# Operands of a Strassen-Winograd projection formed from PSUM, and four steps near them moved, in a one-core decoder block

## The chip, the cores and the metric

The kernel runs on one core of a Trainium2 chip. The metric is the device time of one execution in microseconds (us), as the median of several runs. The core has five engines that run side by side: TensorE (PE, matrix products into PSUM), VectorE (DVE, elementwise), ScalarE (ACT, functions and copies), GpSimd (POOL, elementwise, which in this kernel works on SBUF alone) and SyncE (SP, which here only issues loads and stores). Each engine works through its own instructions in order; they wait for one another through semaphores.

## The reference

One decoder block on x of 1024 positions by 1024 channels, all in float32:

```
u  = RMSNorm(h) * norm_mix_w
P  = u @ w_in                 # [gate_a | gate_s | B_a | C_a | v_a | z | xBC | dt]
A  = (B_a * causal_dwconv3(C_a * v_a)) @ w_a_out
S  = GroupRMSNorm(SSD(silu(conv4(xBC)), softplus(dt + dt_bias)) * silu(z)) @ w_s_out
h  = h + (sigmoid(gate_a) * A + sigmoid(gate_s) * S) @ w_o
v  = RMSNorm(h) * norm_ffn_w
h  = h + (silu(causal_dwconv3(v @ W_1) + b) * (v @ W_3)) @ w_down
out = RMSNorm(h) * final_norm_w
```

SSD is the Mamba-2 scan in chunks of 128 positions: decays are the running sum of dt * a within a chunk, and each chunk uses exp of differences of them.

## The kernel before

**Products.** Every float32 matrix is split in two parts that PE takes quickly: `hi`, the value rounded by an ACT cast, and `lo`, the rest, by a subtraction on DVE or POOL (`split`, L146 to L149). A product of two such operands is three chains of matmuls (`product`, L261): for one 128 x 512 output 12 matmuls of 128 x 512.

**Strassen-Winograd.** The projections by `w_in` (operand U) and by `w_up` (operand V) are computed in pairs of output tiles with seven products in place of eight. The left operand, transposed, is cut into four blocks: A11 and A12 (first 512 positions, lower and upper 512 channels), A21 and A22 (last 512 positions). Four sums are wanted besides A11, A12 and A22:

```
S1 = A21 + A22    S2 = S1 - A11    S3 = A11 - A21    S4 = A12 - S2
```

Each of these is a pair of tiles (hi, lo) of 128 x 4 x 512 (`operand`, L197), filled one row tile of 128 positions at a time. The weights get four sums as well (T1 to T4, `Pair.operands`, L318, all on POOL).

**Filling.** `u_norm(t)` (L436) scales the row tile `xs[t]` in place: ACT squares, DVE makes the mean, POOL the power -0.5, DVE multiplies by it and by the norm weights `nw`, which a DMA has broadcast to all partitions (L433, queued on SP behind the first two rows of x). `fill_first` (L206, t = 0 to 3) transposes eight blocks on PE into two PSUM tiles, splits each from PSUM into A11 and A12, and copies both back into `xs[t]` for later (`keep`, L212). `fill_second` (L214, t = 4 to 7) is a generator in stages: it transposes the row tile, forms S1 with an ACT copy and a DVE addition, copies A21 to SBUF (L236), splits S1 and A22; then S2 = S1 - A11 (L240) and S3 = A11 - A21 (L242), both on SBUF; then S4 (L250), the split of S3 on POOL and the split of S4 on DVE. For V nothing was kept: POOL adds hi and lo of A11 and A12 up again (`whole`, L229).

All operands of U do not fit beside the rows of x: there are 14 large buffers, and S3's and S4's tiles take those of the rows, once these have been read for the last time.

**The order of the work.** The whole program is unrolled; a planner orders the instructions of each engine at build time by a model of their times, in the order of the code where several are ready. `tc.issue_after(i)` ties the instructions traced inside it behind `i` on the same engine. U's phase runs: first halves; the products for dt; second halves; three gate pairs (`head`, L502 to L515) whose first products need A11 and A12 alone; then `then(p)` for each (L679 to L684), s2, s4 and s3 of the pairs interleaved. `so_far` (L328) takes a product out of PSUM, with DVE for these pairs (u2, u3). There is one buffer for T2 (`t2`, L122).

**Decays.** `decays` (L533) makes the decays in a chain on DVE and ACT in [heads, positions], stores them by SP to DRAM for broadcasts, and transposes them on PE into `tk` (L586 to L594). It runs ahead of `BEFORE`, six pairs; its row pool is closed behind it and the pool `ssp` of the SSD chunks opens. A chunk (`ssd_chunk`, L702) loads `m`, the broadcast decays, by a DMA that ACT issues, and makes tables of it with `tk` on ACT (L724). Its stages are called between the products of `BESIDE`, 31 pairs.

**V.** `s_out(1, ..)` (the product by `w_s_out`) calls `fill_first` for V beside its products; `fill_second` runs from the last `out_proj` into the first pairs of the MLP (L1045 to L1094). Then come 22 MLP pairs and the product by `w_down`.

Of the kernel before, what the change touches and what calls it, by code (L numbers as in the profile page):

```python
# [15 lines left out]
P = 128  # L16
# [19 lines left out]
LO_DVE = ("t1", "b22")  # L36

NWAT = 1

# [26 lines left out]
def tile_block(  # L66
# [126 lines left out]


    COMBOS = ("a11", "a12", "a22", "s1", "s2", "s3", "s4")

# [8 lines left out]

    def fill_first(A, v, t, name, keep=False):  # L206

        ts = slice(t * P, (t + 1) * P)
        for pt, c, h in zip(transposed(v, name), ("a11", "a12"), halves):
            split(pt, A[c][0][:, :, ts], A[c][1][:, :, ts], dve)  # L210
            if keep:
                act.copy(blocks(v[:, h]), pt)  # L212

    def fill_second(A, v, t, name, first=None, own=None):  # L214


        pts = transposed(v, f"{name}{t}", mm_tile)
        ts = slice(t * P, (t + 1) * P)

        def put(c, val, eng=dve):  # L220
            split(val, A[c][0][:, :, ts], A[c][1][:, :, ts], eng)

        def whole(c, nm):

            if first is not None:
                return blocks(first[:, halves[c == "a12"]])
            hi, lo = (f32(a[:, :, ts]) for a in A[c])
            o = blocks(c2(f"{nm}{name}{t}"))
            pool.tensor_tensor(o, hi, lo, op=ALU.add)  # L229
            return o  # L230

        s1, a21 = (blocks(v[:, h]) for h in halves)
        act.copy(s1, pts[1])
        dve.tensor_tensor(s1, s1, pts[0], op=ALU.add)
        put("s1", s1)
        act.copy(a21, pts[0])  # L236
        put("a22", pts[1])
        yield
        a11 = whole("a11", "a11")
        dve.tensor_tensor(s1, s1, a11, op=ALU.subtract)  # L240
        put("s2", s1)
        dve.tensor_tensor(a21, a11, a21, op=ALU.subtract)  # L242
        if first is None:
            put("s3", a21, pool)
            yield
        a12 = whole("a12", "a12")
        s4 = a12 if own is None else blocks(
            own.tile([P, HALF], F32, tag="own", name=f"own{name}{t}", bufs=4)
        )
        dve.tensor_tensor(s4, a12, s1, op=ALU.subtract)  # L250
        if first is not None:
            yield
            put("s3", a21, pool)
        put("s4", s4)
        yield
# [5 lines left out]
    def product(ps, c, w, start=True, stop=True, held=False):  # L261


        hi, lo = (t.rearrange("p (k c) -> p k c", k=4) for t in w)
        n = 0
        for wt, ct in ((hi, c[0]), (hi, c[1]), (lo, c[0])):
            for k in range(4):
                pe.matmul(  # L268
                    ps, wt[:, k, :], ct[:, k, :],
                    start=(start and n == 0), stop=(stop and n == 11), skip_group_check=held,  # L270
                )
                n += 1

    class Pair:
# [27 lines left out]
        def first(self, late=False, hold=True, place=None):  # L302


            self.started = True
            p = self.prod("a11", self.r1[:, :HALF], "b11")
            d1 = None if self.d1 is None else self.d1[:, :HALF]
            if place is None:
                place = (d1 if hold else c2(f"m1{self.name}"), d1)
            self.m1, self.c11 = place  # L310
            act.copy(self.m1, p)
# [6 lines left out]
        def operands(self):  # L318
# [3 lines left out]
            self.t1, self.t2, self.t3, self.t4, self.b22 = b11, t2(f"t2{name}"), b12, b21, b22  # L322
            pool.tensor_tensor(self.t1, b12, b11, op=ALU.subtract)
            pool.tensor_tensor(self.t2, b22, self.t1, op=ALU.subtract)
            pool.tensor_tensor(self.t3, b22, b12, op=ALU.subtract)
            pool.tensor_tensor(self.t4, b21, self.t2, op=ALU.subtract)

        def so_far(self, o, c, w, nm):  # L328

            if self.hold:  # L330
                act.copy(o, self.prod(c, w, nm, self.u))
            else:
                dve.tensor_tensor(o, self.m1, self.prod(c, w, nm), op=ALU.add)
                self.m1 = o

# [87 lines left out]
    zeros = const([P, 4], "zeros")  # L423
    dve.memset(zeros, 0.0)
    nw = s4("nw_mix")[:, :DM]
    xs = []
    for t in range(0, NCH, 2):
        xt = big_tile(f"x{t}", shape=(P, 2, DM))
        for i in range(2):
            sp.dma_start(xt[:, i, :], x[(t + i) * P : (t + i + 1) * P, :])  # L430
            xs.append(xt[:, i, :])
            if t + i == NWAT:
                sp.dma_start(nw, norm_mix_w.unsqueeze(0).to_broadcast([P, DM]))  # L433
    U = operand("u")
# [63 lines left out]
    for t in range(4, 8):  # L498
        u_norm(t)
    fills = [fill_second(U, xs[t], t - 4, "u", xs[t - 4], cur["row"]) for t in range(4, 8)]  # L500
    stage(fills[:2])
    for j in range(0, 6, 2):  # L502
# [25 lines left out]
    wns = const([P, NH // 2], "wns", ssd_norm_w)  # L528
    ones = const([P, P], "ones")
    dve.memset(ones, 1.0)  # L530


    def decays(ps):  # L533
# [50 lines left out]
        )  # L584

        tkf = tk.rearrange("p a c q h -> p (a c q h)")  # L586
        for b, arrs in enumerate(((ac, dtv), (dd,))):
            w = len(arrs) * QT
            pt = sd_tile(f"tkp{b}")[:, :w]
            for a, arr in enumerate(arrs):  # L590
                for c in range(2):
                    o = (2 * a + c) * P
                    pe.transpose(pt[:, o : o + P], arr[:, c * P : (c + 1) * P], ident)
            act.copy(tkf[:, b * HALF : b * HALF + w], pt)  # L594


# [82 lines left out]
    for i, p in enumerate(head):  # L679
# [170 lines left out]

    for item in BEFORE:
        run(*item)
    clock[0] = 0
    for item in BESIDE:
# [178 lines left out]
    def fill_beside(j):  # L1033
        if j % 2 == 0:
            fill_first(V, v_norm(j // 2), j // 2, f"v{j // 2}")

    V = operand("v")
    mg = s_out(1, ys1, fill_beside)
    load_x(1)
    V.update(operand("v", False))  # L1040
    def v_second(t):
        v = v_norm(t)
        return fill_second(V, v, t - 4, "v")

# [50 lines left out]


    scf = mkpool("scf", 1)
    two = {}
# [259 lines left out]
```

## Time and profile before

| | |
|---|---|
| runs | 1977.09, 1970.45, 1973.09 us; median 1973.09 |
| profiled execution | 1974.46 us, of which the profile's span is 1972.7 |
| granted clock of TensorE, mean | 0.989 |
| DVE / ACT / POOL busy | 65% / 49% / 63% |
| first transposition on PE | at 10.11 us |
| first product of a gate pair | at 29.36 us |
| first pair of BEFORE | at 101.60 us |
| first product of the MLP | at 1314.55 us |

In the profile's rows, L12 is line 12 of the kernel, `out<-in` are tile names without buffer numbers, and x4 is the number of instructions. The arrow behind an idle time names what ended it. Times in a timeline count from the span's start. PE's matmuls are pipelined, so the time from one start to the next is what one costs. Idle time of an engine that isn't the bottleneck costs nothing.

### The profile page before, as it was taken

The page shows a single profiled execution, that of the slowest core. Times are in us where ns is not written, and L with a number is a line of the kernel's source. Part 1 is how long each engine was busy: PE and PEld are TensorE (multiplying, and loading weights), DVE is VectorE, ACT ScalarE, POOL GpSimd, SP SyncE. Part 2 cuts the span into 40 slices and gives each one's busy share as a digit, 9 for nine tenths or more (in the row PEclk, how much of TensorE's full clock was granted, in tenths as well). Part 3 has the DMA queues.
Part 4 walks back from the last instruction along what each step waited for, and adds up shares of the span by engine and source line. Part 5 has one row for each costly group of instructions (what it writes and reads, how often), then busy time and mean ns, then how long its engine had stood idle before and what let it go on. Part 6 is the DMA issues. An engine that isn't in the chain of part 4 may idle for free.

```text
span 1972.7 us, 25409 instructions
## 1 busy us (share of the span) xinstructions
PE 1914.5 (97%) x8986; PEld 1572.0 (80%) x8986; DVE 1289.6 (65%) x1429; ACT 962.0 (49%) x1636; POOL 1236.3 (63%) x915
## 2 busy tenths in 40 slices
PE   7899999999999999999999999998999999999998
PEld 6678887787788778888888888876888888878886
DVE  8655567767776777777664833479854655585555
ACT  6345457677546664443542323354344444453334
POOL 6657776866776776676445533458876787845342
PEclk9899999999999999999999999998999999999999
DMA  4133355545445554443998974451323344487653
GB/s 166 54 111 121 122 164 172 162 150 190 155 133 164 164 164 124 146 157 110 382 376 279 356 250 161 161 170 35 136 80 108 101 150 163 139 285 264 206 188 143
DMA packets 180175, 338.42 MB, mean 172 GB/s; under 512 B 15280, under 2 KB 87760, under 8 KB 179024
## 3 DMA queue, kind: packets, MB, share of 16 engines
q1 hardware_dynamic: 93264, 253.95, 37.7%
q10 hardware_dynamic: 86784, 82.85, 13.1%
q8 instruction: 70, 1.15, 0.2%
q14 instruction: 57, 0.47, 0.1%
HBM read 247.34 MB, written 89.41 MB: 171 GB/s over the span
## 4 chain that ended last, share of the span: by engine, by line
PE 80%; DVE 7%; ACT 4%; issue 3%; DMA 3%; POOL 2%; ACTq 1%; SPq 0%; POOLq 0%; DVEq 0%
PE pb11up L268 10%; PE so L268 9%; PE pt1up L268 6%; PE pb11xb L268 5%; PE ya L268 4%; PE pb11cv L268 4%; PE d L1151 3%; PE d L1153 3%; PE d L1152 3%; PE pb11z L268 3%; PE pb21up L268 3%; PE pb11ba L268 2%; PE pt1cv L268 2%; PE pt1xb L268 2%; DMA m<-acd 2%
## 5 line engine op out<-in xcount | busy, mean ns | idle before, releaser
L608 DVE SCALAR_TENSOR_TENSOR cv<-xbc,scw,cv 128x1024 f32<-128x1024 f32 x72 | 122.6, 1704 | 46.3 <-ACT cv L604 45.0
L608 DVE SCALAR_TENSOR_TENSOR h<-fci,fcw,h 128x1024 f32<-128x1024 f32 x44 | 85.9, 1953 | 74.1 <-ACT h L604 73.3
L724 ACT ACTIVATE m<-m,tk 128x128 f32<-128x128 f32 x256 | 79.1, 390 | 95.3 <-DMA m<-acd 91.4
L149 POOL TENSOR_TENSOR l_ws<-raw_ws,h_ws 128x512 fp32r<-128x512 f32 x32 | 46.3, 1447 | 71.1 <-PE so L268 40.8
L148 ACT CAST h_ws<-raw_ws 128x512 fp32r<-128x512 f32 x64 | 39.9, 623 | 96.8 <-PE so L268 69.3
L268 PE MATMUL so<-yh,h_ws 128*128 128x512 f32 x256 | 69.0, 391 | 0.0
L268 PE MATMUL so<-yl,h_ws 128*128 128x512 f32 x256 | 68.6, 389 | 0.0
L268 PE MATMUL so<-yh,l_ws 128*128 128x512 f32 x256 | 68.5, 389 | 0.0
L148 ACT CAST h_wo<-raw_wo 128x512 fp32r<-128x512 f32 x48 | 29.7, 621 | 60.3 <-PE wo L985 32.7
L808 DVE TENSOR_TENSOR eb<-eb 128x256 f32<-128x256 f32 x32 | 28.1, 879 | 45.6 <-ACT eb L806 45.6
L149 DVE TENSOR_TENSOR l_ws<-raw_ws,h_ws 128x512 fp32r<-128x512 f32 x32 | 25.1, 785 | 50.0 <-PE so L268 25.5
L149 POOL TENSOR_TENSOR l_wo<-raw_wo,h_wo 128x512 fp32r<-128x512 f32 x24 | 32.3, 1346 | 39.1 <-PE wo L985 30.7
L268 PEld LDWEIGHTS so<-yh,l_ws 128*128 128x128 f32 x256 | 48.0, 188 | 10.0
L268 PEld LDWEIGHTS so<-yl,h_ws 128*128 128x128 f32 x256 | 48.0, 188 | 10.0
L268 PEld LDWEIGHTS so<-yh,h_ws 128*128 128x128 f32 x256 | 47.8, 188 | 9.7
L1128 DVE TENSOR_TENSOR h<-h 128x1024 f32<-128x1024 f32 x22 | 48.7, 2212 | 9.8 <-ACT h L1127 9.6
L314 DVE TENSOR_TENSOR fci<-fci,pb21up 128x512 f32<-128x512 f32 x18 | 12.4, 688 | 60.3 <-PE pb21up L268 60.3
L149 POOL TENSOR_TENSOR l_t3up<-raw_2up,h_t3up 128x512 fp32r<-128x512 f32 x22 | 30.3, 1376 | 32.7 <-PE pb11up L268 32.7
L984 PE MATMUL wo<-l_wo,mh 128*128 128x512 f32 x128 | 50.0, 391 | 0.0
L983 PE MATMUL wo<-h_wo,mh 128*128 128x512 f32 x128 | 49.9, 391 | 0.0
L985 PE MATMUL wo<-h_wo,ml 128*128 128x512 f32 x128 | 49.7, 391 | 0.0
L1127 ACT ACTIVATE h<-h 128x1024 f32<-128x1024 f32 x22 | 23.4, 1062 | 52.7 <-DVE h L608 52.7
(1125 smaller groups left out, 6571.8 us busy)
## 6 DMA issues: line engine op xcount, KB each, us to landing
m<-acd ACTq DMA_DIRECT2D x32, 512.0 KB, 3.9
raw_ws<-in_w_s_out SPq DMA_DIRECT2D x32, 512.0 KB, 4.7
ssd_in<-cv ACTq DMA_DIRECT2D x24, 512.0 KB, 3.1
in<-ssd_in ACTq DMA_DIRECT2D x32, 384.0 KB, 3.8
raw_wo<-in_w_o SPq DMA_DIRECT2D x24, 512.0 KB, 3.8
wd<-in_w_down SPq DMA_DIRECT2D x22, 512.0 KB, 7.0
td<-wd SPq DMA_DIRECT2D x44, 256.0 KB, 4.3
raw_2up<-in_w_up SPq DMA_DIRECT2D x22, 512.0 KB, 3.4
```

The lines of the kernel that those rows point to most:

```text
L148: act.copy(hi, v)
L149: (eng or pool).tensor_tensor(lo, v, f32(hi), op=ALU.subtract)
L268: pe.matmul(ps, wt[:, k, :], ct[:, k, :], start=(start and n == 0), stop=(stop and n == 11), skip_group_check=held,)
L608: dve.scalar_tensor_tensor(cv, ci[:, j : j + SEQ], w[:, j : j + 1], cv, op0=ALU.mult, op1=ALU.add)
L724: act.activation(m[:, h, :], m[:, h, :], AF.Relu, bias=a)
L983: pe.matmul(pss[t], mh, wh, start=k == 0, stop=False)
L984: pe.matmul(pss[t], mh, wl, start=False, stop=False)
L985: pe.matmul(pss[t], ml, wh, start=False, stop=k == NK - 1)
L1128: dve.tensor_tensor(cv, cv, h3, op=ALU.mult)
L1151: pe.matmul(ps, aa[0][:, ts], bb[0], start=k == 0, stop=False)
L1152: pe.matmul(ps, aa[0][:, ts], bb[1], start=False, stop=False)
L1153: pe.matmul(ps, aa[1][:, ts], bb[0], start=False, stop=k == KF - 1)
```

## The change

1. The norm weights come as one row of 4 KB into one partition, first on SP, and two matmuls with a row of ones spread them over the partitions in PSUM; DVE copies them out. `ones` is made at the start.
2. `fill_first` keeps A11 and A12 differently: for U the first block is copied out of PSUM by DVE, the second by ACT, and the second's lo part is POOL's, from the copy. For V an ACT copy keeps A11 in four tiles of a pool of their own, closed when V is done.
3. `fill_second` forms S3 = A11 - A21 and S2 = A22 - S3 on DVE straight from the PSUM tiles, in its first stage; S2 lies where A11 was kept. The copy of A21 is gone, and for V the sum that POOL made of A11. In U the split of S4 gets a stage of its own.
4. T2 of the second gate pair lies in a `c2` buffer. U's last stage, the split of S4, is called between s2 and s3 of the first gate pair, tied on DVE behind that s2's addition.
5. `decays` stops before its transposes; they are called after the third pair of `BEFORE`, tied on PE behind that pair's last matmul. The row pool is closed, and `ssp` opened, after `BEFORE`.

```diff
-    def fill_first(A, v, t, name, keep=False):
+    def fill_first(A, v, t, name, keep=()):
         ts = slice(t * P, (t + 1) * P)
-        for pt, c, h in zip(transposed(v, name), ("a11", "a12"), halves):
-            split(pt, A[c][0][:, :, ts], A[c][1][:, :, ts], dve)
-            if keep:
-                act.copy(blocks(v[:, h]), pt)
+        for n, (pt, c) in enumerate(zip(transposed(v, name), ("a11", "a12"))):
+            hi, lo = (a[:, :, ts] for a in A[c])
+            act.copy(hi, pt)
+            if n < len(keep) and n:
+                act.copy(keep[n], pt)
+                pool.tensor_tensor(lo, keep[n], f32(hi), op=ALU.subtract)
+            else:
+                dve.tensor_tensor(lo, pt, f32(hi), op=ALU.subtract)
+                if n < len(keep):
+                    (dve.tensor_copy if len(keep) == 2 else act.copy)(keep[n], pt)
 
-    def fill_second(A, v, t, name, first=None, own=None):
+    def fill_second(A, v, t, name, a11, a12=None, own=None):
...
-        s1, a21 = (blocks(v[:, h]) for h in halves)
+        s1, s3 = (blocks(v[:, h]) for h in halves)
         act.copy(s1, pts[1])
         dve.tensor_tensor(s1, s1, pts[0], op=ALU.add)
         put("s1", s1)
-        act.copy(a21, pts[0])
         put("a22", pts[1])
+        dve.tensor_tensor(s3, a11, pts[0], op=ALU.subtract)
+        s2 = a11
+        dve.tensor_tensor(s2, pts[1], s3, op=ALU.subtract)
         yield
-        a11 = whole("a11", "a11")
-        dve.tensor_tensor(s1, s1, a11, op=ALU.subtract)
-        put("s2", s1)
-        dve.tensor_tensor(a21, a11, a21, op=ALU.subtract)
-        if first is None:
-            put("s3", a21, pool)
+        put("s2", s2)
+        if own is None:
+            put("s3", s3, pool)
             yield
-        a12 = whole("a12", "a12")
-        s4 = a12 if own is None else blocks(
-            own.tile([P, HALF], F32, tag="own", name=f"own{name}{t}", bufs=4)
-        )
-        dve.tensor_tensor(s4, a12, s1, op=ALU.subtract)
-        if first is not None:
+            s4 = blocks(c2(f"a12{name}{t}"))
+            hi, lo = (f32(a[:, :, ts]) for a in A["a12"])
+            pool.tensor_tensor(s4, hi, lo, op=ALU.add)
+            dve.tensor_tensor(s4, s4, s2, op=ALU.subtract)
+        else:
+            s4 = blocks(own.tile([P, HALF], F32, tag="own", name=f"own{name}{t}", bufs=4))
+            dve.tensor_tensor(s4, a12, s2, op=ALU.subtract)
             yield
-            put("s3", a21, pool)
+            put("s3", s3, pool)
+            yield
         put("s4", s4)
         yield
...
+    ones = const([P, P], "ones")
+    dve.memset(ones, 1.0)
+    nwr = wp.tile([P, 1024], F32, tag="raw", name="nw_row", bufs=NRAW)[:1, :DM]
+    sp.dma_start(nwr, norm_mix_w.unsqueeze(0))
     nw = s4("nw_mix")[:, :DM]
+    for n, h in enumerate(halves):
+        pw = mm_tile(f"nw{n}")
+        pe.matmul(pw, ones[:1, :], nwr[:, h], start=True, stop=True)
+        dve.tensor_copy(nw[:, h], pw)
...
-            if t + i == NWAT:
-                sp.dma_start(nw, norm_mix_w.unsqueeze(0).to_broadcast([P, DM]))
...
+    def kept(v):
+        return [blocks(v[:, h]) for h in halves]
+
     for t in range(4):
         u_norm(t)
-        fill_first(U, xs[t], t, f"u{t}", True)
+        fill_first(U, xs[t], t, f"u{t}", kept(xs[t]))
...
-    for p in head[:2]:
-        p.operands()
+    for i, p in enumerate(head[:2]):
+        p.operands((t2, c2)[i])
...
         p.done = lambda p=p, i=i: gates_done((p.d1, p.d2), gad, 2 * i)
-        then(p)
+        if i == 0:
+            last[0] = p
+            p.s2()
+            with tc.issue_after(mark["dve"]):
+                stage(fills)
+            p.s3()
+        else:
+            then(p)
...
-    decays(dt_ps)
-    rows_.close()
-    ssp = mixer.enter_context(tc.tile_pool(name="ssp", bufs=1))
+    dec = decays(dt_ps)
+    next(dec)
...
-    for item in BEFORE:
+    for n, item in enumerate(BEFORE):
         run(*item)
+        if n == 2:
+            with tc.issue_after(mark["pe"]):
+                next(dec)
+    rows_.close()
+    ssp = mixer.enter_context(tc.tile_pool(name="ssp", bufs=1))
...
+    kept_ = ExitStack()
+    kp = kept_.enter_context(tc.tile_pool(name="kp", bufs=1))
+    v11 = [blocks(kp.tile([P, HALF], F32, name=f"v11{t}")) for t in range(4)]
```

More of the change, by code (lines that the diff above doesn't have):

```diff
@@ L36 @@
 LO_DVE = ("t1", "b22")
-NWAT = 1
 BEFORE = (
@@ L189, in transposed @@
         return pts
+    mark = {}
     COMBOS = ("a11", "a12", "a22", "s1", "s2", "s3", "s4")
@@ L221, in put @@
             split(val, A[c][0][:, :, ts], A[c][1][:, :, ts], eng)
-        def whole(c, nm):
-            if first is not None:
[L226 to L230, printed above, removed]
-        s1, a21 = (blocks(v[:, h]) for h in halves)
+        s1, s3 = (blocks(v[:, h]) for h in halves)
         act.copy(s1, pts[1])
@@ L267, in product @@
             for k in range(4):
-                pe.matmul(
+                mark["pe"] = pe.matmul(
                     ps, wt[:, k, :], ct[:, k, :],
                     start=(start and n == 0), stop=(stop and n == 11), skip_group_check=held,
-                )
+                ).ins
                 n += 1
@@ L310, in first @@
             self.m1, self.c11 = place
-            act.copy(self.m1, p)
+            mark["act"] = act.copy(self.m1, p).ins
             self.hold, self.u = hold, p if hold else None
@@ L316, in first, with operands @@
                 self.operands()
-        def operands(self):
+        def operands(self, place=t2):
             name = self.name
@@ L321, in operands @@
             (b11, b21), (b12, b22) = ([r[:, h] for h in halves] for r in (r1, r2))
-            self.t1, self.t2, self.t3, self.t4, self.b22 = b11, t2(f"t2{name}"), b12, b21, b22
+            self.t1, self.t2, self.t3, self.t4, self.b22 = b11, place(f"t2{name}"), b12, b21, b22
             pool.tensor_tensor(self.t1, b12, b11, op=ALU.subtract)
@@ L330, in so_far @@
             if self.hold:
-                act.copy(o, self.prod(c, w, nm, self.u))
+                mark["act"] = act.copy(o, self.prod(c, w, nm, self.u)).ins
             else:
-                dve.tensor_tensor(o, self.m1, self.prod(c, w, nm), op=ALU.add)
-                self.m1 = o
+                i = dve.tensor_tensor(o, self.m1, self.prod(c, w, nm), op=ALU.add)
+                mark["dve"], self.m1 = i.ins, o
         def s2(self):
@@ L499, in tile_block @@
         u_norm(t)
-    fills = [fill_second(U, xs[t], t - 4, "u", xs[t - 4], cur["row"]) for t in range(4, 8)]
+    fills = [fill_second(U, xs[t], t - 4, "u", *kept(xs[t - 4]), cur["row"]) for t in range(4, 8)]
     stage(fills[:2])
@@ L528, in tile_block @@
     wns = const([P, NH // 2], "wns", ssd_norm_w)
-    ones = const([P, P], "ones")
-    dve.memset(ones, 1.0)
     def decays(ps):
@@ L584, in decays @@
         )
+        yield
         tkf = tk.rearrange("p a c q h -> p (a c q h)")
@@ L594, in decays @@
             act.copy(tkf[:, b * HALF : b * HALF + w], pt)
+        yield
     def ssd_slot(t):
@@ L688, in tile_block @@
     dt_add(dt3, "a22", (2, 3))
-    decays(dt_ps)
-    rows_.close()
-    ssp = mixer.enter_context(tc.tile_pool(name="ssp", bufs=1))
+    dec = decays(dt_ps)
+    next(dec)
+    ssp = None
     def heads(t):
@@ L1034, in fill_beside @@
         if j % 2 == 0:
-            fill_first(V, v_norm(j // 2), j // 2, f"v{j // 2}")
+            fill_first(V, v_norm(j // 2), j // 2, f"v{j // 2}", v11[j // 2 : j // 2 + 1])
     V = operand("v")
+    kept_ = ExitStack()
+    kp = kept_.enter_context(tc.tile_pool(name="kp", bufs=1))
+    v11 = [blocks(kp.tile([P, HALF], F32, name=f"v11{t}")) for t in range(4)]
     mg = s_out(1, ys1, fill_beside)
@@ L1042, in v_second @@
         v = v_norm(t)
-        return fill_second(V, v, t - 4, "v")
+        return fill_second(V, v, t - 4, "v", v11[t - 4])
     out_proj(mg, 4, 2)
@@ L1094, in tile_block @@
         stage(g)
+    kept_.close()
     scf = mkpool("scf", 1)
```

1 line of the change is left out of this document (removed).

## The prediction

> **What bounds the kernel.** I read the page first: one profiled execution, with the busy time of TensorE (PE) and its granted clock in 40 slices of 49.3 us.
>
> ```profile
> span 1972.7 us, 25409 instructions
> PE 1914.5 (97%) x8986; PEld 1572.0 (80%) x8986; DVE 1289.6 (65%) x1429; ACT 962.0 (49%) x1636; POOL 1236.3 (63%) x915
> PEclk9899999999999999999999999998999999999999
> ```
>
> PE is the bound, and the change takes no matrix product away. So only time in which PE stands idle or runs at a lower clock can be won: 58 us of idle in the span, and the two slices with an 8 in the clock row. Where they lie is shown by the view of windows, cut at the stages (PE busy, then PEld, DVE, ACT, POOL, clock, DMA share, GB/s).
>
> ```profile
> 30.00:82.00 52.00, 44.65 (x194) 35.78 (x193) 44.58 (x45) 25.18 (x47) 40.14 (x29) 0.90 0.09 29
> 160.00:1320.00 1160.00, 1147.18 (x5611) 939.82 (x5610) 766.90 (x903) 593.21 (x1065) 726.80 (x543) 1.00 0.57 191
> 1320.00:1370.00 50.00, 39.13 (x154) 31.46 (x153) 49.91 (x42) 20.88 (x38) 41.99 (x28) 0.86 0.10 34
> ```
>
> The long middle is tight (12.8 us idle in 1160). Two short stretches hold 18 us of idle and the lower clock: 30 to 82, where the operands of the first projection are made, and 1320 to 1370, where those of the MLP are. In the second DVE is busy for 49.9 of 50 us: there VectorE is the bound. The view of waits for PE names each stop (us in total, times, longest); I asked it for 0 to 160 and for 1320 to 1372.
>
> ```profile
> PE pt2g L268 <- DVE u2g L333: 3.9, 1, 3.9
> PE pb11xb L268 <- ACT u3xb L331: 2.3, 1, 2.3
> PE tkp L593 <- DVE ee L559: 2.0, 1, 2.0
> PE pt2g L268 <- DVE us2l L149: 1.9, 1, 1.9
> PE pt1g L268 <- DVE us1l L149: 1.0, 1, 1.0
> PE pb11z L268 <- ACT u3z L331: 1.0, 1, 1.0
> ...
> PE pt_v L187 <- DVE h L1009: 3.9, 1, 3.9
> PE pt1up L268 <- DVE vs1l L149: 3.9, 1, 3.9
> PE pt2up L268 <- DVE vs2l L149: 3.1, 1, 3.1
> ```
>
> A stop costs more than its length, because PE comes back slow. The chain of work that ended last (start, us, what), and two stretches of PE's timeline, show it:
>
> ```profile
> 74.26 5.49 PE pt2g L268 x12
> ...
> 81.86 2.72 PE pt1g L268 x12
> ...
> 1362.99 3.66 PE pt2up L268 x8
> ```
> ```profile
> 62.53 1.78 PE L268 MATMUL pt2g<-us2h,l_t2g 128*128 128x512 f32 x4
> 64.11 1.91 PE L268 MATMUL pt3g<-us3h,h_t3g 128*128 128x512 f32 x4
> 65.82 0.53 PE L481 MATMUL ps_dt<-us1l,wdt10h 128*128 128x256 f32 x2
> ...
> 120.95 1.91 PE L268 MATMUL pb11xb<-us3l,h_t3xb 128*128 128x512 f32 x4
> 122.66 0.63 PE L268 MATMUL pb11xb<-us3h,l_t3xb 128*128 128x512 f32 x1
> ```
>
> Twelve matmuls take 2.72 us at full clock (0.227 each) and 5.49 after the stop of 3.9: 2.8 lost. In the same way eight take 3.29 from 62.53 to 65.82 (1.5 lost, after the stop of 1.9), and eight 3.66 at 1362.99 (1.8 lost, after the stop of 3.1; for the 3.9 before vs1l I take 1.7, between these two); after the tkp stop four take 1.71 where 0.91 is usual (0.8 lost there, and the matmuls on both sides are part slow: I take 1.3).
>
> [...]
>
> **The change part by part.**
>
> *Formed from PSUM (U).* While DVE makes the second half of U, its operations have these times (busy us, mean ns | idle before):
>
> ```profile
> L149 DVE TENSOR_TENSOR us4l<-ownu,us4h 128x512 fp32r<-128x512 f32 x4 | 6.8, 1760 | 3.7 <-POOL us3l L149 3.7
> ...
> L240 DVE TENSOR_TENSOR x<-x,x 128x512 f32<-128x512 f32 x4 | 5.4, 1353 | 0.0
> L242 DVE TENSOR_TENSOR x<-x,x 128x512 f32<-128x512 f32 x4 | 4.9, 1229 | 0.0
> ...
> L234 DVE TENSOR_TENSOR x<-x,pt_u 128x512 f32<-128x512 f32 x4 | 2.7, 680 | 0.6 <-ACT x L233 0.6
> ```
>
> L234 has one operand in PSUM and takes 0.68 each time. L240 and L242 (S2 and S3, both operands in SBUF) average 1.35 and 1.23 though they are as large, and the four S4 splits 1.76; the long ones lie beside POOL's subtractions, the short ones beside none. The change makes L240 and L242 into operations on a PSUM tile: eight of 0.68, 5.4 instead of 10.3, so DVE's row of work, which has no idle in between, is 4.9 us shorter when it reaches us2l. The stops for us1l and us2l (1.0 and 1.9) and the slow matmuls behind the second (1.5) are 4.4. Four ACT copies of the second block go too; ACT isn't the bound here. The price: a transposed tile stays in PSUM for two more DVE operations, 1.4 us, and the next transposes may wait for it. Bounds: +1.4 to -5.5 (the 4.4 and 1.1 of small stops). I take **-4.2**.
>
> [...]
>
> *First half of U.* For each of the four rows one ACT copy of a transposed half becomes a DVE copy, one DVE subtraction goes to POOL, and ACT loses its copies' time (first row below: busy us, mean ns). POOL has room, but a scale of x, a DVE operation with two SBUF operands, can then meet a subtraction of POOL (second row, the tile view: lowest/median/highest ns):
>
> ```profile
> L212 ACT COPY x<-pt_u 128x512 f32<-128x512 f32 x7 | 4.2, 653 | 0.0
> ```
> ```profile
> L179 DVE SCALAR_TENSOR_TENSOR x<-x,r_x,nw_mix x8: 1276/1280/2304, 8.8 to 27.2; 128x1024 f32<-128x1024 f32 x8
> ```
>
> Each meeting costs 1.0. POOL's own queue holds the next row's power behind such a subtraction. Bounds: +4.1 (four meetings) to -2.4 (four ACT copies of 0.6 at their full price). I take **+0.5**, one meeting against a gain of half a microsecond.
>
> *Norm weights.* Now the first scale waits for a 512 KB broadcast, and the third row of x comes behind that broadcast on SP's queue:
>
> ```profile
> 4.64 1.06 ACT L174 ACTIVATE sq<-x 128x1024 f32<-128x1024 f32 x1 [2.56 <-DMA x<-in_x]
> ...
> 8.77 2.48 DVE L179 SCALAR_TENSOR_TENSOR x<-x,r_x,nw_mix 128x1024 f32<-128x1024 f32 x2 [1.58 <-DMA nw_mix<-in_norm_mix_w]
> 10.10 1.06 ACT L174 ACTIVATE sq<-x 128x1024 f32<-128x1024 f32 x1 [3.09 <-DMA x<-in_x]
> ```
> ```profile
> L783 PE MATMUL pst<-xe,bk x56: 590/592/697, 272.6 to 895.1; 128*128 128x512 f32 x56
> 0.00:30.00 30.00, 17.58 (x99) 15.85 (x100) 21.71 (x42) 21.47 (x44) 12.38 (x21) 0.89 0.76 272
> ```
>
> The new load is 4 KB and goes first on SP, so every load of x is issued one issue later (0.4). Two fp32 matmuls and two DVE copies (0.68) must end before the first scale. The matmul isn't in the trace with one row of weights; the nearest, pst, has two records of 0.59 in each, so at most 1.2, twice that on a slow clock, 4.8 for two. The first row of x is there at 4.6, so the new row, a hundredth of its size, by then at the latest: the first scale starts by 4.6 + 4.8 + 1.4 = 10.8, 2.0 later than now, or, if the matmuls run while x still comes, as early as the wait of 1.6 allows. At 272 GB/s the 512 KB not moved bring the third row forward by 1.9. Bounds: +2.0 to -1.9. I take **-1.0**, the wait of 1.6 less the later issue, for the chain runs from these two through ACT, DVE and POOL to the first products.
>
> *T2 apart and S4 later (U).* On DVE the four S4 splits (6.8, above) stand ahead of u2g, which frees the PSUM bank that the next pair's pt2g wants. That is the stop of 3.9, and 2.8 of slow matmuls: 6.7. After the change the splits stand behind u2g, with ACT's casts behind this pair's. Behind them on DVE now wait u3g and the gate sum of the same pair, and pt3g of the next pair wants u3g's bank. That is what is late next. The splits still can't start before POOL's us3l is done (3.7 idle). A second T2 tile lets POOL fill the time it now spends waiting for the only one:
>
> ```profile
> L149 POOL TENSOR_TENSOR l_t2g<-t2g,h_t2g 128x512 fp32r<-128x512 f32 x2 | 2.6, 1291 | 4.1 <-ACT h_t2g L148 4.1
> ```
>
> So POOL reaches us3l up to 3.3 earlier (two subtractions of about 1.65), unless DVE's S4 and S2 come later. If the splits again take 6.8, a new stop of up to 4.1 (6.8 less the 2.7 of the next pair's s2, which PE then has ready) stands in place of the old. Bounds: 0 to -6.7. I take **-4.0**, most of it but with a new stop of about 1.5 and its slow matmuls.
>
> *Decays transposed later.* The transposes wait on PE for a chain of DVE operations, and hold the ready products up: 2.0 and 1.3. Three pairs of seven products later (some 57 us at 2.72) the operands are long there. So **-3.3**. And ACT, whose next work is the decay tables:
>
> ```profile
> 133.95 0.40 ACT L724 ACTIVATE m<-m,tk 128x128 f32<-128x128 f32 x1 [6.53 <-DMA m<-acd]
> ```
>
> It waits 6.5 us for the broadcast of m with u3xb queued behind; that is PE's stop of 2.3 and, with the tables run after it, the one of 1.0. The row pool now stays in use until the transposes after the third pair have read it, so the pool that m lies in opens later, and its loads (two of m, then inputs) move with it on ACT's queue. The wait is moved, not removed, and what is queued behind it then may or may not be wanted by PE. Bounds: -3.3 to +3.3. I take **-1.1**. SP's queue keeps its stores of the decays in place.
>
> *V.* The same in the MLP's operand, where DVE bounds:
>
> ```profile
> L240 DVE TENSOR_TENSOR h<-h,a11v 128x512 f32<-128x512 f32 x4 | 6.3, 1564 | 0.0
> L242 DVE TENSOR_TENSOR h<-a11v,h 128x512 f32<-128x512 f32 x4 | 6.0, 1496 | 0.0
> ```
> ```profile
> L229 POOL TENSOR_TENSOR a11v<-va11h,va11l 128x512 f32<-128x512 f32 x4 | 6.8, 1741 | 0.0
> ```
>
> Of DVE's 12.3 the half for rows 4 and 5 moves ahead, beside out_proj, where PE is full; the other half stays at 4 x 0.68 = 2.7. DVE is 9.6 us shorter before the last vs2l, and POOL loses four sums of 6.8 us in all (A11 is kept), which also were what DVE's operations met. The stops for vs1l (3.9 + 1.7) and vs2l (3.1 + 1.8) are 10.5. The stop of 3.9 for the last row's norm (L1009) stands ahead of all this and stays. Cost: four ACT copies of 0.6 beside w_s_out (hidden by PE at a full 1160 us; 2.4 if not), and four DVE operations of 0.68 in out_proj's tail (0 to +2.7; I take 0, as DVE waits for PE there). Bounds: +2.7 to -10.5. I take **-7.5**, a stop of about 1.5 and its slow matmuls being left.
>
> **The sum.** -4.2 + 0.5 - 1.0 - 4.0 - 3.3 - 1.1 - 7.5 = -20.6. The profiled execution took 1974.5 us (span 1972.7 and 1.8 around it), 1.4 above the median of the three runs, 1973.1. From the median the sum gives 1952.5; I say **1952**.
>
> **The rivals.**
>
> *Order only* (0.15): the code fixes an order on one engine, and the planner lays the S4 splits and the transposes so that the same buffers are late as before; T2 apart, S4 and decays give nothing (8.4 less). Speaks for it: u3g takes u2g's place behind the splits. Time 1961.
>
> *All stops go* (0.14): DVE's shorter row also lets go the stop of 3.9 for L1009 and the slow matmuls behind it (at most the 2.8 seen after u2g), and the terms reach their bounds of -5.5, -6.7, -6.6 and -10.5; with -0.5 for the head that is -32 to -37. Against it: L1009 waits for things that the change doesn't touch. Time about 1939.
>
> *No gain* (0.10): POOL takes DVE's place. us3l comes when S2's splits too are done, since S2 now lies in the kept block and its buffer is handed on, and the two fills gain under 6 us together. Time 1968 to 1975.
>
> *Slower* (0.05): m's wait moves into the steady stretch. Each wait of ACT ahead of a copy that PE needs costs a stop like 2.3 and more; there are 32 chunks, and from 9 such stops on (9 x 2.3 = 20.7) the sum is eaten up; with 16 the time is 1989. Against it: from the third chunk on m's two buffers are handed on by the chunk before, not by the row pool, so two chunks are moved at most.
>
> **How the numbers follow.** The forecast itself, -11 to -28, has 0.56. Time 1952. Low is 1940, at the second rival; high 1967, at the edge of what a measurement tells from no change (0.3% is 5.9 us). Left out: half of the second rival's lower side, no gain, slower, some 0.2. Faster 0.85 (forecast, order only, all stops), same 0.10, slower 0.05.
>
> **What would show it.** S2 and S3 on DVE at 0.68 for every record; no wait of PE for u2g, tkp, vs1l or vs2l; no a11v on POOL; the wait for L1009 still at 3.9; the windows 30 to 82 and 1320 to 1370 some 8 and 7 us shorter for the same matmul counts. I am wrong if the middle (160 to 1320) gains or loses more than 5 us, if PE waits for us4l, u3g or us3l for more than 3 us in place of u2g, or if ACT's wait for m shows up as stops of PE after the sixth pair.

## The result, and the profile after

The changed kernel took 1947.22 us (median of 4 runs, 1945.36 to 1949.44) against 1972.94 us beside it: ratio 0.987, 95% interval 0.9856 to 0.9883, a gain of 25.7 us where 21 were forecast. A second measurement gave 1946.66 us; below, 1946.9, the middle of the two, stands for the changed kernel. Its profiled execution took 1947.18 us. One execution of the experiments below, the profiled one of e5, ran in a disturbed state (2758.28 us at a granted clock of 0.649) and is left out. The page of the changed kernel (span; busy us of each engine; granted clock of PE in 40 slices):

```profile
span 1945.5 us, 25405 instructions
...
PE 1907.6 (98%) x8990; PEld 1567.3 (81%) x8990; DVE 1280.5 (66%) x1431; ACT 958.6 (49%) x1630; POOL 1238.5 (64%) x915
...
PEclk9999999999999999999999999999999999999999
```

PE's work is the same but for four records (the norm weights' two matmuls), the span is 27 us shorter, and no slice is left with an 8 in the clock row. The view of windows of the changed kernel, the two short ones cut to the same counts of matmuls as in the prediction and the middle to the same width (columns as there):

```profile
29.00:74.60 45.60, 40.68 (x194) 33.07 (x193) 39.67 (x43) 20.28 (x38) 39.65 (x28) 1.00 0.04 12
...
145.00:1305.00 1160.00, 1148.24 (x5616) 940.63 (x5616) 775.33 (x910) 605.02 (x1093) 724.62 (x542) 1.00 0.57 192
...
1304.00:1343.60 39.60, 36.25 (x154) 29.13 (x154) 34.84 (x37) 18.30 (x36) 34.34 (x24) 0.91 0.11 40
```

The same 194 matmuls take 45.6 us instead of 52.0, the 154 of the MLP's start 39.6 instead of 50.0, and the long middle is as tight as it was. To see where the rest comes from, take the first product of each stage from PE's timeline (start, us, what). Before:

```profile
29.36 0.94 PE L268 MATMUL pb11g<-ua11h,h_b11g 128*128 128x512 f32 x3
...
101.60 0.63 PE L268 MATMUL pb11xb<-ua11h,h_b11xb 128*128 128x512 f32 x2
...
271.57 0.66 PE L770 MATMUL pd<-m,xd 128*64 128x128 f32 x8
...
1002.96 1.07 PE L268 MATMUL so<-yh,h_ws 128*128 128x512 f32 x4
...
1744.51 0.39 PE L1151 MATMUL d<-d10h 128*128 128x512 f32 x1
```

After:

```profile
28.34 1.17 PE L268 MATMUL pb11g<-ua11h,h_b11g 128*128 128x512 f32 x4
...
94.19 1.09 PE L268 MATMUL pb11xb<-ua11h,h_b11xb 128*128 128x512 f32 x4
...
256.33 0.88 PE L788 MATMUL pd<-m,xd 128*64 128x128 f32 x12
...
987.01 1.07 PE L268 MATMUL so<-yh,h_ws 128*128 128x512 f32 x4
...
1717.84 0.39 PE L1178 MATMUL d<-d10h 128*128 128x512 f32 x1
```

The differences between neighbouring rows are the lengths of four stages. They are the ruler for all experiments: U (72.24 before, 65.85 after), the decays (169.97, 162.14), the SSD (731.39, 730.68) and V with the MLP's first half (741.55, 730.83). So the change won 6.4 in U, 7.8 at the decays, 10.7 in V, 0.7 in the SSD, 1.0 in the head before the first row and 0.5 behind the last, which makes up the 27.2 of the span (the last three are no larger than what these pieces vary by from trace to trace).

The view of waits of the changed kernel for PE, first for 29 to 160, shows which stops are left (us in total, times, longest):

```profile
PE pt3g L268 <- ACT gt L354: 2.1, 1, 2.1
PE pt3g L268 <- DVE u3g L333: 1.7, 1, 1.7
PE pt3g L268 <- POOL l_t3g L147: 0.6, 1, 0.6
PE pt2g L268 <- DVE us2l L147: 0.5, 1, 0.5
```

and for 1290 to 1350:

```profile
PE pt1up L268 <- DVE vs1l L147: 2.6, 1, 2.6
PE pt4up L268 <- ACT h_t4up L146: 0.7, 1, 0.7
```

The stops for us1l, u2g, tkp, u3xb, u3z, vs2l and the last row's norm are gone, and that for us2l is down from 1.9 to 0.5. Two larger new ones stand in U, and vs1l is still waited for.

### The profile page after: what moved, and what is told of

It reads as the page before. It is cut to its first block, busy times and chain, and to the rows that moved or that the text cites. A ratio compares the mean times of both kernels' runs of the same rounds, so it can differ in the third digit from the quotient of the medians.

```text
span 1945.5 us, 25405 instructions
## 1 busy us (share of the span) xinstructions
PE 1907.6 (98%) x8990; PEld 1567.3 (81%) x8990; DVE 1280.5 (66%) x1431; ACT 958.6 (49%) x1630; POOL 1238.5 (64%) x915
## 4 chain that ended last, share of the span: by engine, by line
PE 83%; DVE 5%; ACT 4%; DMA 3%; issue 3%; POOL 2%; ACTq 1%; SPq 0%; POOLq 0%; DVEq 0%
PE pb11up L268 9%; PE so L268 9%; PE pb11xb L268 6%; PE pt1up L268 5%; PE ya L268 5%; PE pb11cv L268 4%; PE pb11z L268 4%; PE d L1178 3%; PE d L1180 3%; PE d L1179 3%; PE pb21up L268 2%; PE pt1xb L268 2%; PE pb11ba L268 2%; PE pt1cv L268 2%; PE pt1g L268 2%
## 5 line engine op out<-in xcount | busy, mean ns | idle before, releaser
L147 DVE TENSOR_TENSOR l_ws<-raw_ws,h_ws 128x512 fp32r<-128x512 f32 x32 | 25.5, 796 | 50.9 <-PE so L268 21.4
L1155 DVE TENSOR_TENSOR h<-h 128x1024 f32<-128x1024 f32 x22 | 47.1, 2140 | 10.3 <-ACT h L1154 10.1
L770 DVE TENSOR_TENSOR m<-m,cb 128x1024 f32<-128x1024 f32 x32 | 48.6, 1518 | 0.6
```

The lines of the kernel that those rows point to most:

```text
L147: (eng or pool).tensor_tensor(lo, v, f32(hi), op=ALU.subtract)
L770: dve.tensor_tensor(m, m, cb.unsqueeze(1).to_broadcast([P, HG, P]), op=ALU.mult)
```

## The experiments

Each kernel undoes one part of the change in the changed kernel, unless said otherwise. Times are medians of four or five runs. The ratios, with their 95% intervals, are to the kernel before, which ran again beside each group of kernels (medians 1972.94, 1972.45, 1972.44 and 1971.78, of 4 to 9 runs); the row "before" is the middle of these. The stages as defined above, in us, from each kernel's own trace:

| kernel | time | ratio | less 1946.9 | U | decays | V |
|---|---|---|---|---|---|---|
| before | 1972.4 | 1 | +25.5 | 72.24 | 169.97 | 741.55 |
| after | 1947.22 | 0.9856 to 0.9883 | | 65.85 | 162.14 | 730.83 |
| after again (e13) | 1946.66 | 0.9852 to 0.9887 | | 66.77 | 162.12 | 731.12 |
| e1 decays early | 1954.29 | 0.9895 to 0.9925 | +7.4 | 66.66 | **168.73** | 730.94 |
| e2 S4 early, one T2 | 1949.99 | 0.9872 to 0.9905 | +3.1 | **68.98** | 162.09 | 730.95 |
| e3 V as before | 1957.19 | 0.9905 to 0.9935 | +10.3 | 66.86 | 162.28 | **741.44** |
| e4 head as before | 1946.78 | 0.9853 to 0.9883 | -0.1 | 65.96 | 162.15 | 730.93 |
| e5 ACT tied | 1948.5 | 0.9855 to 0.9888 | +1.6 | no trace | no trace | no trace |
| e6 S2, S3 of U from SBUF, later | 1956.31 | 0.9901 to 0.993 | +9.4 | **76.94** | 162.17 | 730.91 |
| e7 S2, S3 of V from SBUF, later | 1949.10 | 0.9867 to 0.9896 | +2.2 | 66.88 | 162.13 | **733.01** |
| e8 one T2 | 1945.95 | 0.9852 to 0.9884 | -1.0 | 65.37 | 162.12 | 731.46 |
| e10 as e6, in after's place | 1949.75 | 0.9873 to 0.9906 | +2.9 | **71.20** | 162.16 | 731.22 |
| e11 as e7, in after's place | 1951.14 | 0.9875 to 0.9912 | +4.2 | 65.91 | 162.17 | **735.08** |
| e12 one T2 and the old head | 1945.88 | 0.9846 to 0.9883 | -1.0 | 66.04 | 162.19 | 731.13 |

Of these three stages each edit moves its own alone. Between kernels whose edit doesn't touch U that stage scatters by 1.0 us, the decays by 0.2 and V by 0.6. The SSD, which no edit touches, scatters far more, from 727.60 (e3) to 732.33 (e6); so a stage tells more than the time of its one profiled execution.

**e1: the decays transposed at once.**

```diff
-    dec = decays(dt_ps)
-    next(dec)
-    ssp = None
+    for _ in decays(dt_ps):
+        pass
+    rows_.close()
+    ssp = mixer.enter_context(tc.tile_pool(name="ssp", bufs=1))
...
-        if n == 2:
-            with tc.issue_after(mark["pe"]):
-                next(dec)
-    rows_.close()
-    ssp = mixer.enter_context(tc.tile_pool(name="ssp", bufs=1))
```

> The changed kernel (1947.2 us) with the decays transposed where they were before, and the row pool closed there; all else as changed. Theory (the step of the prediction, -3.3 -1.1): the stop for the transposes comes back and a third of ACT's stops, +4.4 us, 1951.6. Rival, read from the trace of after, where PE has no stop at all between 73 and 300 us: all of ACT's stops behind its wait for m hung on the early transposes, +7 to +8 us, 1954 to 1955, with stops of PE for tkp, u3xb and u3z in the profile.

It cost 7.4 us, as the rival had it and not the theory. The waits of PE in e1, 100 to 160:

```profile
PE pb11xb L268 <- ACT u3xb L331: 2.2, 1, 2.2
PE tkp L602 <- DVE ee L567: 2.1, 1, 2.1
```

and ACT's timeline in e1 (the wait in brackets):

```profile
124.69 0.40 ACT L741 ACTIVATE m<-m,tk 128x128 f32<-128x128 f32 x1 [6.42 <-DMA m<-acd]
124.99 0.56 ACT L331 COPY u3xb<-pb11xb 128x512 f32<-128x512 f32 x1
```

ACT sits 6.4 us in front of the table of m, and the copy of u3xb, which PE wants, stands right behind it. The same place in the changed kernel, ACT's timeline:

```profile
152.28 0.36 ACTq L733 DMA_DIRECT2D m<-acd  x1
...
157.75 2.45 ACT L742 ACTIVATE m<-m,tk 128x128 f32<-128x128 f32 x8
```

The load is issued at 152.28 and used at 157.75 with no wait for it shown. In between ACT makes three copies and a cast and waits 1.5 us for PE and 1.6 for a load of weights, and none of this stops PE. So ACT's first wait for m wasn't moved, it was covered: up to 300 us ACT waits three times for m in e1, 13.5 us in all, and twice after, 6.7, and these two stop PE in neither. The stop for u3z (1.0 before) isn't back in e1. By PE's timeline the two stops are 4.3, and the sixteen matmuls from 125.61 to 131.00 take 5.4 us instead of 3.6; that is 6.1 of the 6.6 by which the stage is longer. About 2 of it belong to tkp and 4 to m. e1 puts both the transposes and the opening of m's pool back; the two weren't tried apart.

**e2 and e8: S4 and T2.** e2 is both, e8 the T2 tile alone:

```diff
             put("s3", s3, pool)
-            yield
         put("s4", s4)
...
-        p.operands((t2, c2)[i])
+        p.operands()
...
-        if i == 0:
-            last[0] = p
-            p.s2()
-            with tc.issue_after(mark["dve"]):
-                stage(fills)
-            p.s3()
-        else:
-            then(p)
+        then(p)
```

> The changed kernel with the split of S4 called where it was before (ahead of s2 of the first gate pair, in one stage with that of S3) and one T2 buffer for both pairs; all else as changed. Theory (the step of the prediction): +4.0 us, 1951.2, with the stop for u2g of 3.9 back. Rival, by the stops that stand in the trace of after in its place (2.1 for gt L354, 0.6 for l_t3g, 1.7 for u3g): the step is worth only about 2 us, 1949. Second rival: with DVE's row shorter than before, the early S4 split would not be late at all, 1947 or less.

> The changed kernel with one T2 buffer for both gate pairs; all else as changed. Theory (the step of the prediction): POOL waits 4.1 us for the only T2 tile again and reaches us3l up to 3.3 us later, +1 to +2 us, 1948 to 1949. Rival: in after us3l waits for DVE's us2l and not for POOL's row, so nothing changes: within 0.7 us of 1947.2.

e2 cost 3.1 (between its theory and its first rival), e8 nothing that can be measured (-1.0, its interval covers that of the changed kernel). Between e2 and e8, which differ in the place of S4 alone, lie 4.0 us in time and 3.6 in the stage. The waits of PE in e2, 28 to 82:

```profile
PE pt2g L267 <- DVE u2g L332: 2.8, 1, 2.8
PE pt3g L267 <- POOL us3l L147: 1.8, 1, 1.8
```

The stop for u2g is back, but at 2.8, not 3.9. The two stops that the changed kernel has in its place are 2.1 and 1.7, so moving S4 exchanged stops of 4.6 for stops of 3.8. Part of the rest is in what follows them: the eight matmuls behind e2's stop for u2g take 3.5 us (69.07 to 72.53) instead of 1.8. In the first profile of the changed kernel those behind the two new stops are not slow (four take 1.20 behind the first, 1.16 behind the second); in the second (e13) the stop for u3g is 1.0, but the eight matmuls behind the other take 3.4 (last section). So a part of this difference varies from one execution to the next, and stage U is 3.1 and 2.2 longer in e2 than in these two profiles.

**e5: the first of the new stops.** ACT's copy for pt4g stands behind three casts of S4 that wait for POOL; e5 ties the casts behind the copy:

```diff
-            act.copy(self.d1[:, HALF:], self.prod("a22", self.t4, "t4"))
+            mark["t4"] = act.copy(self.d1[:, HALF:], self.prod("a22", self.t4, "t4")).ins
...
-            with tc.issue_after(mark["dve"]):
+            with tc.issue_after(mark["dve"]), tc.issue_after(mark["t4"]):
                 stage(fills)
```

> The changed kernel with the S4 split's ACT casts tied too: behind ACT's copy of pt4 (L354), which in the trace of after stands behind three such casts while these wait 7.1 us for POOL's us3l, and whose lateness is PE's stop of 2.1. Theory: that stop goes, -1.5 to -2.5 us, 1945, if the casts, then later, do not make u3g later by as much. Rival: the stop moves to u3g (1.7 in after), since the S4 split's DVE part ends later: within 0.7 us of 1947.2.

The median is 1948.5 us, ratio 0.9872 (0.9855 to 0.9888): the gain of the theory isn't there. These runs left no trace, so whether the stop went and what took its place stays open.

**e4 and e12: the head.** e4 loads the norm weights by the old broadcast and fills the first half as before; e12 is e4 with e8's single T2 tile:

```diff
-    nwr = wp.tile([P, 1024], F32, tag="raw", name="nw_row", bufs=NRAW)[:1, :DM]
-    sp.dma_start(nwr, norm_mix_w.unsqueeze(0))
...
-        pe.matmul(pw, ones[:1, :], nwr[:, h], start=True, stop=True)
-        dve.tensor_copy(nw[:, h], pw)
...
+            if t + i == 1:
+                sp.dma_start(nw, norm_mix_w.unsqueeze(0).to_broadcast([P, DM]))
...
-            if n < len(keep) and n:
-                act.copy(keep[n], pt)
-                pool.tensor_tensor(lo, keep[n], f32(hi), op=ALU.subtract)
...
```

> The changed kernel with the norm weights broadcast by a DMA behind the second row of x and the first half of U kept as before (both copies on ACT, both lo parts on DVE); all else as changed. Theory (the steps of the prediction, +0.5 -1.0): +0.5 us, 1947.7; from the first product of a gate pair, 1.0 earlier in after than before, +1.0. Rival: POOL's four subtractions delay the U rows more than the weights gain, so undoing both is a gain: 1945 to 1947.

> One T2 tile and the head as before the change, both together: each alone measured -0.4 and -1.3. If these are real and add, 1.7 below the changed kernel of this call (about 1945.5); if they are chance or overlap, within 1 us of it.

Neither differs from the changed kernel by more than 1.0 us, less than these runs can tell apart; e12's question stays open. The scales do start earlier, as forecast: in the changed kernel DVE's timeline has

```profile
7.55 1.28 DVE L177 SCALAR_TENSOR_TENSOR x<-x,r_x,nw_mix 128x1024 f32<-128x1024 f32 x1
```

where it was 8.77 before. But the first product doesn't come earlier for it: 28.34 and 27.08 in the two profiles of the changed kernel (26.92 to 28.34 in all ten profiles with the new head), 26.19 in e4 and 26.24 in e12 with the old head, 29.36 in the kernel before, whose head is the old one too. Much of the spread comes with the clock: before, the small products ahead of it take 0.63 us a pair until 24.9 (granted clock 0.50 from 20 to 25) and 0.40 from 25.25 on (0.99 from 25 to 30); in e4 they take 0.40 from 19.7 on.

**e6 and e10: S2 and S3 of U from SBUF.** Both copy the second block to SBUF first, as before the change. e6 also forms S2 and S3 where the old code did, after the first step of all rows; e10 leaves them at the changed kernel's place and in its buffers (e10 shown):

```diff
+        if own is not None:
+            act.copy(s3, pts[0])
         put("a22", pts[1])
...
+        if own is not None:
+            dve.tensor_tensor(s3, a11, s3, op=ALU.subtract)
+            s2 = a11
+            dve.tensor_tensor(s2, s1, a11, op=ALU.subtract)
+        else:
...
```

> The changed kernel with S2 and S3 of U alone formed as before, from SBUF copies (ACT copies A21, S2 = S1 - A11, S3 = A11 - A21); V and all else as changed. Theory (the step of the prediction): the eight DVE operations are long again (10.3 us instead of 5.4) and PE stops for us1l and us2l again, +4.2 us, 1951.4. Rival: the later S4 and the second T2 tile already take the pressure off DVE and POOL, so it costs under 2 us.

> S2 and S3 of U are formed from an SBUF copy of the second block (four ACT copies more), but at the place and into the buffers of the changed kernel. If it is the source that counts (two SBUF operands that can meet POOL), several of the eight operations take 1.2 to 1.8 us in place of 0.68 and the time is about +4.2 (1951 to 1953). If it is the place in DVE's order that counts (the sums of S1 not held up, which is what e6 lost), the time is within +1.5 of the changed kernel, and PE has no stop for us1h.

e10 cost 2.9 us by its median, between its two forecasts. Its profiled execution took 1952.04 (its five runs 1949.17 to 1952.95), and stage U there is 5.4 and 4.4 longer than in the two profiles of the changed kernel. The groups of DVE (24 to 62) of e10 (busy us, mean ns | idle before):

```profile
L239 DVE TENSOR_TENSOR x<-x,x 128x512 f32<-128x512 f32 x4 | 6.0, 1494 | 0.0
...
L241 DVE TENSOR_TENSOR x<-x,x 128x512 f32<-128x512 f32 x4 | 4.3, 1068 | 0.0
```

and of the changed kernel:

```profile
L238 DVE TENSOR_TENSOR x<-pt_u,x 128x512 f32<-128x512 f32 x4 | 2.7, 677 | 0.0
L236 DVE TENSOR_TENSOR x<-x,pt_u 128x512 f32<-128x512 f32 x4 | 2.7, 675 | 0.0
```

The eight operations take 10.3 us with both operands in SBUF and 5.4 with one in PSUM: the 4.9 of the prediction to a tenth. PE's largest wait in e10 shows where they are paid:

```profile
PE pt1g L275 <- ACT us1h L146: 4.8, 1, 4.8
```

The sum S1 of the last row stands behind them on DVE. ACT's four extra copies are not what is late: its cast us1h had waited 4.9 us for that sum. The source thus counts, and the rival that it is only the place is out. e6 cost 9.4, more than twice its theory: this stop is 5.7 there, the one for u3g has grown to 3.2, and the stage is 4.7 us longer than even before the change. The old place doesn't go with S4's new one; why it doesn't wasn't tried.

The single operations show it too: all eight forms with a PSUM operand take 0.67 to 0.68 in the changed kernel, beside a POOL that is busy for 23.1 of 23.1 us (25.6 to 48.7), while those of e10, beside a POOL that is busy for 23.0 of 23.1 us (28 to 51.1), go from 0.68 to 1.78.

**e3, e7 and e11: V.** e3 puts V's whole fill back (no kept A11, POOL's sums, the old place). e7 keeps A11 but forms S2 and S3 from SBUF in the old place; e11 forms them from SBUF in the new place. The edits of e7 and e11 are those of e6 and e10 with `own is None`; the core of e3:

```diff
-        return fill_second(V, v, t - 4, "v", v11[t - 4])
+        return fill_second_old(V, v, t - 4, "v")
...
+        act.copy(a21, pts[0])
+        put("a22", pts[1])
+        yield
+        a11 = whole("a11", "a11")
+        dve.tensor_tensor(s1, s1, a11, op=ALU.subtract)
+        put("s2", s1)
+        dve.tensor_tensor(a21, a11, a21, op=ALU.subtract)
```

> The changed kernel with the MLP's operand V filled as before (A11 summed up again by POOL, S2 and S3 from SBUF), U and all else as changed. Theory (the step of the prediction): the stops for vs1l and vs2l come back, +7.5 us, 1954.7, and the stop for the last row's norm (L1009 before) is as absent as in after, as it has nothing to do with the change. Rival: the whole difference of the two traces in this stretch, 9.8 us, belongs to V's fill, the norm's stop included: 1957, with that stop of 3.9 back.

> The changed kernel with S2 and S3 of V alone formed from SBUF copies as before, but A11 still kept, so POOL's four sums of A11 stay away. Theory (DVE bounds V's stretch, and forming from PSUM is what shortens its row): most of V's part comes back, +5 to +7 us, 1952 to 1954. Rival: POOL's four sums (6.8 us), which met DVE's operations, were the cost: within 2 us of 1947.2.

> The same for V alone. If the stop for the last row's norm went because of the place of S2 and S3 in the order (the norm chain and so POOL's operand subtractions come later, DVE's splits of the first pair ahead of them), it stays away here, vs1l stops PE for some 2.6 us as in the changed kernel, and the time is within 1.5 of it. If it went because the operations read PSUM, the stop of 4 us for pt_v is back, and the time is +2 or more.

e3 gives back 10.3 us, nearly all of V, as its rival had it, with the norm's stop. The waits of PE (1290 to 1350) in e3:

```profile
PE pt_v L185 <- DVE h L1064: 3.9, 1, 3.9
PE pt1up L300 <- DVE vs1l L147: 3.6, 1, 3.6
PE pt2up L300 <- DVE vs2l L147: 3.0, 1, 3.0
```

In e7:

```profile
PE pt_v L185 <- DVE h L1039: 6.3, 2, 4.5
```

In e11, from the whole span:

```profile
PE pt2up L275 <- DVE vs2l L147: 4.6, 1, 4.6
...
PE pt_v L185 <- DVE h L1039: 2.2, 1, 2.2
```

Keeping A11 alone (e3 to e7) ends both stops for the operand and 8.1 us, though S2 and S3 are still formed from SBUF. What went was POOL's four sums, and with them the wait for these: in e7 four of the eight operations are done by 1295.9, beside out_proj, where in e3 the first starts at 1313.86; and of the other four, three take 0.67 to 0.68, in or right behind a pause of 3.8 us on POOL. Which of the two counts for more wasn't tried. The stop for the norm stays in e7. So e7's rival came near, and not its theory. The new place with SBUF forms (e11: the time of its second forecast, but a stop of 2.2 and not of 4) shortens the norm's stop but makes vs2l late, and is 2.0 slower than e7. Only with the PSUM forms in the new place, in the changed kernel, are both gone. The price stands at vs1l, which e7 doesn't wait for. PE's timeline after:

```profile
1325.85 1.19 PE L268 MATMUL pt1up<-vs1l,h_t1up 128*128 128x512 f32 x4 [2.62 <-DVE vs1l L147]
...
1329.32 2.07 PE L268 MATMUL pt4up<-va22h,h_t4up 128*128 128x512 f32 x4 [0.73 <-ACT h_t4up L146]
1331.19 1.91 PE L268 MATMUL pt4up<-va22l,h_t4up 128*128 128x512 f32 x4
```

How the norm's stop went is seen on POOL and DVE. Before, POOL's timeline:

```profile
1317.20 0.55 POOL L1008 TENSOR_TENSOR r_v<-rs_v,nhalf 128x1 f32<-128x1 f32 x1 [0.67 <-DVE rs_v L1006]
1317.71 2.54 POOL L323 TENSOR_TENSOR raw_1up<-raw_2up,raw_1up 128x512 f32<-128x512 f32 x2
```

and DVE's:

```profile
1326.35 1.75 DVE L149 TENSOR_TENSOR l_b21up<-fx,h_b21up 128x512 fp32r<-128x512 f32 x1
1328.03 2.28 DVE L1009 SCALAR_TENSOR_TENSOR h<-h,r_v,nw_ffn 128x1024 f32<-128x1024 f32 x1
```

After, DVE's:

```profile
1306.71 0.68 DVE L147 TENSOR_TENSOR l_b21up<-fx,h_b21up 128x512 fp32r<-128x512 f32 x1
1307.83 2.30 DVE L1032 SCALAR_TENSOR_TENSOR h<-h,r_v,nw_ffn 128x1024 f32<-128x1024 f32 x1 [0.44 <-POOL r_v L1031]
```

POOL's subtractions of the first pair are tied behind the last r_v. Before, r_v came first, the subtractions ran, and DVE's splits of the later pairs' weights (fx), slow beside them (1.18 to 1.78 us each), stood between r_v and the scale: 10.8 us from the one's start to the other's. After, the last r_v starts at 1306.87, when those splits are done at 0.68 each, and the scale follows 1.0 later. In e11 it is 5.0, in e7 11.3. That the order makes the difference is read from these four traces; it wasn't tried by itself.

> The changed kernel itself, as the base of this call: 1947 within 1.5 us.

1946.66 us, as expected: e10, e11 and e12 have the same base as the others.

## Why the prediction was right, and where it was not

The forecast of -20.6 was right in sign and in most of its steps, and 5 short. The two short windows became 6.4 and 10.4 us shorter for the same matmuls, where it said 8 and 7. U gave less than its two terms, V and the decays more. By its terms, against what undoing each cost (the sum of these, 23.6, is near the 25.5 of the whole, since the terms lie in different stages or behind each other):

| term | forecast | undone alone |
|---|---|---|
| S2 and S3 of U from PSUM | -4.2 | -2.9 (e10; its stage 4.4 to 5.4) |
| norm weights and first half of U | -0.5 | 0.1 (e4) |
| T2 apart, S4 later | -4.0 | -3.1 (e2) |
| decays later, with m's wait | -4.4 | -7.4 (e1) |
| V | -7.5 | -10.3 (e3) |

**Formed from PSUM (U):** right, in the operations (4.9 us of DVE) and nearly in the size. The stops for us1l and us2l went as forecast, but for 0.5. Undone alone the time is paid elsewhere, at us1h, so the near agreement in size says nothing of these two stops. An operation that reads PSUM took no longer than an SBUF form at its shortest: means of 675 and 677 ns here, 0.67 to 0.69 for the shortest SBUF forms (e7).

**Head:** the early scale came (1.2 earlier, 1.0 taken), but the step from there to the first products failed. PE then waited 2.9 and 2.0 us (in the two profiles) for ACT's cast wdt22h, and the start of the first product varies by 1.4 us under the same head (26.92 to 28.34), more than the term: PE's small products ahead of it take 0.40 us a pair from 23.24 on in the first profile, from 21.79 on in the second.

**T2 and S4:** S4's new place is right, in kind and nearly in size: the new stop was named at u3g and found there at 1.7 (1.0 in e13), and between e2 and e8 it is worth 4.0, though a part of that varies with the slow matmuls. A second one, for ACT's copy of pt4g, wasn't seen: the prediction had ACT's casts of S4 behind this pair's, and in the trace three of the four stand ahead of that copy. T2 apart is worth nothing: POOL started us3l when DVE's us2l let it (an idle of 1.23 at 57.26), not when T2 came free, which is the reservation that the prediction made ("unless DVE's S4 and S2 come later").

**Decays:** right in mechanism for the transposes, not for m. The prediction held that the wait for m "is moved, not removed", and took a third of its bound. It was covered, and all of PE's stops behind it went: about 4 us in e1, against 1.1. The transposes gave about 2 in e1, against 3.3, since no slow matmuls followed their stop there (the next two groups of four take 1.17 and 1.08, where it was 1.32 and 1.91 before). That the bounds of both (3.3 and 3.3) add up to the 6.6 by which e1's stage grew is chance.

**V:** right in the sum by luck, and in half the mechanism. "The stop of 3.9 for L1009 stays" fell: it went, with the 2.7 that the slow matmuls behind it cost (PE's timeline before, 1330.36 to 1336.61), 6.6 us that the sum didn't have. The operand's two stops, priced at 7.5, gave less. vs2l's 3.1 went with 1.6 of slow matmuls. But vs1l, which was to shrink to 1.5, stayed at 2.6; with a second stop of 0.7 and 3.2 of slow matmuls behind both it costs 6.5 in the first profile after, and 4.3 (2.7 and 1.6) in the second, against 5.5 before (3.9 and 1.6). So of V's 10.7 the norm's stop gave some 6.6, and the operand's two stops 4 to 6 where 7.5 was forecast. What ended the operand's stops in e7 was the kept A11, with SBUF forms; the PSUM forms and the new place together ended the norm's.

The middle held (1.1 us less idle in its window), no stop for u3g was over 3 us, and no rival came: no wait of ACT for m stops PE after the sixth pair. Of the signs named ahead two failed, those for vs1l and L1009. "All stops go" has its first half, the norm's stop, but not its time of 1939 (its terms add up to -34 to -37 with that stop, not -32).

## What to carry to other kernels

Where DVE and POOL work side by side, count the DVE operations with both operands in SBUF: reading one from PSUM shortened them here (10.3 to 5.4 us), and so did taking POOL's own work away by keeping a value (e7, where V's eight took 7.0 us in place of 12.3, half of them earlier than before). A wait that stands in front of work that others want is worth moving to a place where its engine has work of its own to fill it; look there for what is queued behind before pricing it at nothing. Undo each part of a bundle alone: the second T2 tile and the new head moved nothing that could be measured. And add up a stage's stops after the change as well as before: a sum can come out near the result although one of its terms gave less and something outside it made up the difference.

## What the runs showed of the chip that was not expected

Whether a stop is followed by slow matmuls isn't told by its length. PE's timeline in e1, after a stop of 2.20:

```profile
125.61 1.21 PE L268 MATMUL pb11xb<-ua22h,h_t4xb 128*128 128x512 f32 x4 [2.20 <-ACT u3xb L331]
126.66 1.48 PE L268 MATMUL pb11xb<-ua22l,h_t4xb 128*128 128x512 f32 x4
127.94 1.91 PE L268 MATMUL pb11xb<-ua22h,l_t4xb 128*128 128x512 f32 x4
129.64 1.52 PE L268 MATMUL pb11z<-us2h,h_t2z 128*128 128x512 f32 x4
```

in the changed kernel, after 2.07 for pt3g:

```profile
62.01 1.20 PE L268 MATMUL pt3g<-us3h,h_t3g 128*128 128x512 f32 x4 [2.07 <-ACT gt L354]
63.05 1.08 PE L268 MATMUL pt3g<-us3l,h_t3g 128*128 128x512 f32 x4
```

and in the second profile of the same changed kernel (e13), after the same stop:

```profile
61.70 1.92 PE L268 MATMUL pt3g<-us3h,h_t3g 128*128 128x512 f32 x4 [2.07 <-ACT gt L354]
63.41 1.91 PE L268 MATMUL pt3g<-us3l,h_t3g 128*128 128x512 f32 x4
```

Four matmuls take up to 1.91 in the first case (twelve from 125.61 to 129.64, 4.0 us instead of 2.7), 1.20 and 1.08 in the second, and 1.92 and 1.91 in the third, where kernel, place and length of the stop are those of the second. Before, at the product of the first case and after a stop of 2.26, they take 1.20 and 1.08. So the slow matmuls after a stop, which the prediction added to each stop as a fixed part, come or don't, from one execution to the next; what decides it isn't shown. Slow matmuls followed the 2.20 of e1 and the 2.07 of e13, and not the 2.07 of the other profile or the 2.26.
